# Neighbourhood attention in a two-layer backbone: scores as products over 128 stacked rows, or as products over 64 rows per head with both heads in turn

## The chip, the cores and the metric

The kernel runs on one core of a Trainium2 chip. Five engines of that core work in parallel: TensorE (PE in the profile; its weight loads are the rows PEld), VectorE (DVE), ScalarE (ACT), GpSimd (POOL) and SyncE (SP, which issues the DMAs). The metric is the device time of one execution in microseconds; lower is better.

## The reference, cut to what matters

Layer 0 is a differential attention and layer 1 a neighbourhood attention, both over 512 latent tokens and 256 context tokens with D = 1024; only layer 1 is touched by the change. It has 32 heads of 64 features:

```
q = rms_norm(q.reshape(bsz, n, NA_HEADS, NA_DH), qn_g)     # k likewise; v plain; z is the gate
k_band = kr[:, :, band_cols]                               # the keys near a block of queries
s = jnp.einsum('bnqhd,binxhd->bhnqix', q_r, k_band).astype(F32) * scale
s = jnp.where(valid[:, :, None, :], s + bias, -jnp.inf)
s_ctx = jnp.einsum('bnqhd,bkhd->bhnqk', q_r, k_c).astype(F32) * scale
p = jax.nn.softmax(jnp.concatenate([s, s_ctx], axis=-1), axis=-1)
out = einsum(p_band, v_band) + einsum(p_ctx, v_c)
out_l = (o_l * jax.nn.silu(z_l)) @ w_out
```

A block of 128 queries (16 columns of the grid by 8 rows) sees 256 latent keys (32 columns by 8 rows) and the 256 context keys. All is float32.

## The kernel before

**Numbers in two parts.** TensorE is used in the type fp32r. Each float32 operand is kept as a rounded part hi and a rest lo, and a product a·b is taken as hi·hi + hi·lo + lo·hi.

**Groups.** Layer 1 works in 16 groups of two heads (128 features). For each group `b_project` makes queries, keys, values and gate from the modulated tokens u (tiles `uhi`, `ulo`) and the group's weights (`whi`, `wlo`): 24 products a tile of 128 tokens, named `pj`. The weights come by DMA into `wraw`; ACT casts `whi` from it, and `wlo` = `wraw` - `whi` is made by DVE for half of them and by POOL for the other half. The tokens stand in three halves of 256: context (half 0), and two latent ones.

**Queries and keys.** DVE scales them by 1 / rms: `put_q` writes each head's 64 query features twice side by side (tile `qd`), `put_k` the keys once (tile `kk`). TensorE transposes them into the PSUM tiles `pq` and `pk`, so that features lie on partitions. `q_transposed` splits `pq` into `qT` [128, hi / lo, head, 256]: since a head's features were doubled, its 128 partitions hold the same 64 numbers twice. `k_transposed` splits `pk` into `KSb` [128, 2, 768], where a head's 128 partitions are hi on 64 and lo on the other 64. So a product over 128 partitions gives q·(k hi + k lo) at once.

**Scores.** `b_scores` runs once for each head (at half steps `s0` and `s1` of a group), with four blocks n of 128 queries each. A block's scores `Sb` fill one PSUM bank of 512 columns: 256 of the band and 256 of the context, each from two products (q hi, q lo), so 4 products of 256 columns a bank. Then DVE adds the bias (`bm`) and takes the row's least value (`nmb`), and ACT takes the exponentials into `pb` (n = 0 and 3) or `pp` (n = 1 and 2). `b_weights` transposes these on TensorE into `pwb`, ACT and DVE split them into `wTb`, and `b_values` multiplies with the values (`oTb`).

**What sets the order.** The program is first noted down as a list (class `Plan`; every instruction is issued from its line 277, so the profile shows L277 throughout). `Plan.order` then runs a list scheduler with estimated durations (`Op.estimate`), and every engine's instructions are issued in the order of that plan. On each engine this order is fixed; engines wait for each other by semaphores. PSUM has 8 banks: two for `pj`, three with tag `m` (`pq`, `pk`, `pwb`, `oTb` and others take turns), three for `Sb`. A new tile waits until the readers of the bank's earlier tile are done.

Of the kernel before, what the change touches and what calls it, by code (L numbers as in the profile page):

```python
# [18 lines left out]
P = 128  # L19
D = 1024  # L20
KT = 8
NG = 16
# [3 lines left out]
# token halves of 256: 0 = context, 1 and 2 = latent  # L26
# [10 lines left out]
# half steps of a projection between the parts of the attention  # L37
LAG = dict(pw=2.5, pv=1.5, po=0.5, py=1.5, qka=2, qkb=3, b1=2, b2=1.5, b3=1, bo=0.5, by=3)
# half steps at which the weights of the next groups are loaded, and the scores of a head begin
AT = dict(a0=8, a1=11, a2=11, a3=0, b0=6, b1=9, b2=9, b3=0, s0=5, s1=7, c0=2, c1=7, sa=0, cg=2, ch=9, c2=9, cv=1)  # L40
# [16 lines left out]
class Pool:  # L57
    """tiles of a pool by tag, with the number of buffers of each tag in one place"""
# [12 lines left out]
# ns from the end of an instruction to the start of one that needs it  # L71
# [12 lines left out]
class Op:  # L84
    """an instruction that waits for its place: its engine, what it touches, what it is likely to take"""
# [8 lines left out]
    def estimate(self, name):  # L94
        """ns"""
# [3 lines left out]
        if e == "PE":  # L99
            return 2.5 + n * (1 if reads[0].dtype == F32R else 2 if name == "transpose" else 4) / 2.4 if n > 2 else 260  # L100
# [15 lines left out]
class Rec:  # L116
    """an engine that notes its instructions"""
# [13 lines left out]
class Plan:  # L131
    """notes the program, then issues every engine's instructions in the order of a simulated run"""
# [48 lines left out]
    def order(self):  # L181
# [21 lines left out]
        def offer(i):  # L203
            """to its engine, unless a buffer is missing"""
# [19 lines left out]
        while len(out) < len(ops):  # L224
# [11 lines left out]
            # two of a tag at once, or a buffer gone since  # L236
# [4 lines left out]
            if e == "PE":  # L241
                # the tensor engine's clock is halved after an idle window
# [37 lines left out]
class K:  # L280
# [3 lines left out]
    # ------------------------------------------------------------ constants  # L284
# [19 lines left out]
    def load_vecs(self):  # L304
        """silu of both conditioning vectors, on every partition"""
# [23 lines left out]
    def mod_first(self):  # L329
        """scale and shift of layer 0 on the tensor engine; two steps per two tiles of features"""  # L330
# [7 lines left out]
        # columns: hi of both vectors, lo of both; their sums are the products with the weights' hi and lo  # L338
# [53 lines left out]
    def first_u(self, x, v, u, n, half):  # L392
        """two tiles of features of u hi / lo from x / rms"""
# [12 lines left out]
    def scaled(self, x, s, half):  # L406
        """x / rms, in place"""
# [4 lines left out]
    def mod_chunk(self, layer, ch):  # L412
        """e[:, ch] = (W^T chunk) . silu(c) for both vectors"""
# [9 lines left out]
    def mod_finish(self, layer, v, part):  # L423
        """part 0: shift b, 1: a = g (1 + scale), 2: gate"""
# [20 lines left out]
        # a token to a partition for the power, then to every partition  # L445
# [14 lines left out]
    def make_u(self, x, s, a, b):  # L460
        """x, 1 / rms -> u hi / lo"""
# [36 lines left out]
    def loads(self, Wn, W, layer, g, hs, on_pool):  # L498
        """weights of the next groups: the last part of g + 1 and the others of g + 2"""
# [5 lines left out]
    def project(self, o, W, u, j, kts, c=slice(0, 512)):  # L505
        """one tile of 128 tokens (tile j of a half) x the columns of a group"""
# [10 lines left out]
    # ------------------------------------------------------------ order of work: half steps  # L517
# [3 lines left out]
    def tick(self, step=0.5):  # L521
        """everything that is due by now"""
# [9 lines left out]
    def drained(self, gen, fill, hs):  # L532
        """what is left of the attention, with the steps of other work for the half steps that follow"""
# [7 lines left out]
    # ------------------------------------------------------------ per-head rms of q and k  # L541
# [5 lines left out]
    def rstd(self, sq):  # L547
        """squares [128, 2, 128] -> 1 / rms of each 64 columns, [128, 4]"""
# [8 lines left out]
    def put_q(self, t, rs, dst):  # L557
        """t [128, 128] (two heads) times rs, each head twice, into dst [128, 2, 2, 64]"""
# [9 lines left out]
    def q_transposed(self, qds):  # L568
        """two tiles [128, 2, 2, 64] -> [128, head, hi / lo, 256]"""
# [15 lines left out]
    def k_transposed(self, ks, KS, half):  # L585
        """two tiles [128, 128] -> stacks of hi and lo; head 0: (hi; lo), head 1: (lo; hi)"""
# [9 lines left out]

    def gate_z(self, pz, dst, mul=None):
# [5 lines left out]
    def gained(self, out, x, g):  # L603
        """[128, 2, 128] times a gain [128, 2, 64] of both heads"""
# [3 lines left out]
    def rope(self, ps, t):  # L608
        """(q | k) of a latent tile, rotated and times the norm's gains"""
# [14 lines left out]
    # ------------------------------------------------------------ layer 0: differential attention  # L624
    def a_tables(self):
# [35 lines left out]
    def a_tile(self, G, half, j, ps):  # L661
        """queries, keys, values and gate of a tile of 128 tokens"""
# [37 lines left out]
    def a_scores(self, g, G, half, j):  # L700
        """scores of 128 queries with both heads' keys, softmax and difference of the two"""
# [20 lines left out]
        # l0 (p0 / l0 - lambda p1 / l1); the norm that follows takes l0 out again  # L722
# [67 lines left out]
    # ------------------------------------------------------------ layer 1: neighbourhood attention  # L790
    def b_tables(self):
# [3 lines left out]
        # the scores come out negated: q's gain carries the sign  # L795
# [6 lines left out]
        for i in range(2):  # L802
            t = sb.tile([P, 2, 704], F32, name=f"pp{i}", tag="x8")
            nc.gpsimd.memset(t[:, :, 0:64], 0.0)
            nc.gpsimd.memset(t[:, :, 320:384], 0.0)
            self.pp += [t[:, 0], t[:, 1]]

    def b_project(self, G, U, W):
# [3 lines left out]
        for half in range(3):  # L812
            V = sb.tile([P, 2, 4, 64], F32R, name="Vb", tag="V")
            G["v"][half] = V
            if half == 0:
                # keys and values alone: both tiles share a bank
# [9 lines left out]
                ks = []  # L826
                for j in range(2):
                    ks.append(sb.tile([P, P], F32, name="kk", tag="kk"))
                    self.put_k(t1[:, j], rs[:, 2 * j : 2 * j + 2], ks[j])
                self.b_v(ps[:, :, P:256], V)  # L830
                self.later(LAG['qkb'], self.qk_transposed, G, half, None, ks)
                continue
            qds, ks = [], []
            for j in range(2):
# [14 lines left out]
                qd = sb.tile([P, 2, 2, 64], F32, name="qd", tag="qd")  # L849
                self.put_q(t1[:, 0:128], rs[:, 0:2], qd)  # L850
                qds.append(qd)
                self.gate_z(ps[:, 384:512], Z[:, j])
                k = sb.tile([P, P], F32, name="kk", tag="kk")
                self.put_k(t1[:, 128:256], rs[:, 2:4], k)
                ks.append(k)
                self.b_v(ps[:, 256:384].unsqueeze(1), V[:, j : j + 1])
                if j == 1:
                    self.later(LAG['qkb'], self.qk_transposed, G, half, qds, ks)
                yield

    def b_v_hi(self, ps, V):
        """values [.., 128] -> [.., 4, 64]: head 0: hi | lo, head 1: lo | hi"""
# [6 lines left out]
    def b_bias(self, g, h):  # L869
        """minus the bias, and what masks: one per place of a query block in the row; the last part is for the context"""  # L870
# [4 lines left out]
        for geo in range(3):  # L875
            o = 128 - 64 * geo
            nc.vector.tensor_tensor(bm[:, geo], self.mask[:, geo], raw[:, o : o + 256], ALU.subtract)
        nc.gpsimd.memset(bm[:, 3], 0.0)
        self.bm[h] = bm

    def b_scores(self, g, G, h):
        nc, sb = self.nc, self.sb
        KS, bm = G["KS"], self.bm[h]
        if h == 0:
            G["l"] = sb.tile([P, 4, 2], F32, name="lb", tag="lb")
            G["pair"] = sb.tile([P, 512], F32, name="pair", tag="oT")
        l = G["l"]
        pn = []
        for n in range(4):
            geo = (0, 1, 1, 2)[n]  # L890
            k0 = 256 + (0, 64, 192, 256)[n]
            S = self.psS.tile([P, 512], F32, name="Sb", tag="S")
# [5 lines left out]
            S2 = S.rearrange("p (a b) -> p a b", a=2)  # L898
            nm = sb.tile([P, 1], F32, name="nmb", tag="nm")
# [443 lines left out]
```

## Time and profile before

| | |
|---|---|
| median of 3 runs | 1830.32 us (1828.95 to 1832.27) |
| profiled execution, first to last instruction | 1827.4 us |
| median of the runs less that span | 2.9 us |
| TensorE busy | 1775.6 us, 97% |
| VectorE busy | 1487.5 us, 81% |
| ScalarE busy | 969.8 us, 53% |
| GpSimd busy | 602.2 us, 33% |
| groups of layer 1 | from about 1070 to 1745 us |

The profiled execution's own time is its span; what a run's time holds beyond the span (launch and end) is the 2.9 us. Busy is the union of an engine's instructions. A matmul's row shows from its start to its modelled end, which overlaps the next one's start, so the pace of TensorE is read from the distance of starts, not from the durations.

### The profile page before, as it was taken

What the parts mean: (1) busy time and instruction counts of PE and PEld (TensorE: products, weight loads), DVE (VectorE), ACT (ScalarE), POOL (GpSimd) and SP (SyncE); (2) the same over time, 40 slices, a digit from 0 to 9 for tenths busy, and PEclk for the clock granted to TensorE, in tenths of its full rate; (3) what the DMA queues carried; (4) which work ended last, traced back from release to release, by engine and by line L of the source; (5) the groups of instructions that cost most, each with busy time, mean ns of one, the idle gap of its engine ahead of it and who ended that gap; (6) DMA issues with size and microseconds to landing.
All of it is one profiled execution on the core that took longest, in us unless ns stands there. A gap on an engine that the chain in (4) does not pass through costs nothing.

```text
span 1827.4 us, 29430 instructions
## 1 busy us (share of the span) xinstructions
PE 1775.6 (97%) x10032; PEld 1509.2 (83%) x10032; DVE 1487.5 (81%) x3437; ACT 969.8 (53%) x2654; POOL 602.2 (33%) x915
## 2 busy tenths in 40 slices
PE   7899999999999999999999999999999999999999
PEld 3688888888888888888889988888888888888887
DVE  5888999898999999989858777777777777777863
ACT  4456555555555555556636455555555555555641
POOL 4544434444444444343100123333333333332100
PEclk9899999999999999999999999999999999999999
DMA  7401222121222222223556321111122211111423
GB/s 282 136 15 56 76 79 67 56 71 59 65 78 87 79 79 76 78 72 105 187 156 215 100 78 62 61 61 61 63 70 68 67 61 61 61 61 61 146 95 104
DMA packets 60774, 160.74 MB, mean 88 GB/s; under 512 B 7376, under 2 KB 22096, under 8 KB 59728
## 3 DMA queue, kind: packets, MB, share of 16 engines
q1 hardware_dynamic: 60624, 158.86, 26.7%
q8 instruction: 79, 1.29, 0.3%
q14 instruction: 71, 0.58, 0.1%
HBM read 144.68 MB, written 14.16 MB: 87 GB/s over the span
## 4 chain that ended last, share of the span: by engine, by line
PE 75%; DVE 15%; ACT 5%; issue 2%; POOL 2%; DMA 0%; SPq 0%; DVEq 0%; ACTq 0%; POOLq 0%
PE pj L277 40%; PE pjo L277 12%; PE oT L277 4%; PE S L277 4%; PE Sb L277 3%; PE pwb L277 3%; ACT pexp L277 3%; DVE wlo L277 3%; POOL ms L277 2%; PE pq L277 2%; DVE nm L277 2%; PE pw L277 1%; PE oTb L277 1%; DVE kk L277 1%; DVE t L277 1%
## 5 line engine op out<-in xcount | busy, mean ns | idle before, releaser
L277 PE MATMUL pj<-whi,ufirst 128*128 128x512 f32 x1536 | 524.6, 402 | 2.4 <-ACT ufirst L277 1.9
L277 PEld LDWEIGHTS pj<-whi,ufirst 128*128 128x128 f32 x1536 | 289.9, 189 | 58.1 <-ACT ufirst L277 2.5
L277 PE MATMUL pj<-wlo,ufirst 128*128 128x512 f32 x768 | 303.2, 395 | 0.0
L277 PE MATMUL pj<-wlo,uhi 128*128 128x512 f32 (+1 forms) x768 | 278.5, 363 | 12.1 <-DVE wlo L277 12.1
L277 PE MATMUL pj<-whi,uhi 128*128 128x512 f32 (+1 forms) x768 | 279.5, 364 | 0.0
L277 PE MATMUL pj<-whi,ulo 128*128 128x512 f32 (+1 forms) x768 | 276.3, 360 | 0.0
L277 ACT CAST whi<-wraw 128x512 fp32r<-128x512 f32 x352 | 209.3, 631 | 105.1 <-PE pjo L277 31.5
L277 DVE TENSOR_TENSOR wlo<-wraw,whi 128x512 fp32r<-128x512 f32 x288 | 220.6, 789 | 40.4 <-ACT whi L277 39.5
L277 POOL TENSOR_SCALAR ssk<-ssk 128x4 f32<-128x4 f32 x176 | 35.3, 201 | 556.9 <-DVE ssk L277 555.0
L277 ACT ACTIVATE pexp<-S,nm 128x768 f32<-128x768 f32 (+1 forms) x192 | 144.2, 758 | 127.8 <-DVE nm L277 127.7
L277 PE MATMUL pjo<-yhl,whi 128*128 128x512 f32 (+1 forms) x768 | 208.0, 357 | 0.0
L277 POOL TENSOR_TENSOR rsk<-ssk,mhalf 128x4 f32<-128x4 f32 x176 | 179.7, 1021 | 14.5
L277 PEld LDWEIGHTS pj<-wlo,uhi 128*128 128x128 f32 x768 | 145.2, 189 | 35.6 <-DVE wlo L277 19.0
L277 PEld LDWEIGHTS pj<-wlo,ufirst 128*128 128x128 f32 x768 | 145.8, 190 | 26.5
L277 PEld LDWEIGHTS pj<-whi,ulo 128*128 128x128 f32 x768 | 145.2, 189 | 17.9
L277 PEld LDWEIGHTS pj<-whi,uhi 128*128 128x128 f32 x768 | 145.3, 189 | 15.9
L277 PEld LDWEIGHTS pjo<-yhl,whi 128*128 128x128 f32 x768 | 134.8, 189 | 18.3
L277 DVE TENSOR_TENSOR wTb<-pwb,wTb 128x512 fp32r<-128x512 f32 (+2 forms) x192 | 101.1, 554 | 48.6 <-ACT wTb L277 47.7
L277 DVE TENSOR_REDUCE nm<-S 128x2 f32<-128x1536 f32 (+1 forms) x96 | 134.0, 1396 | 6.1 <-PE S L277 6.0
L277 PE MATMUL pjo<-yhl,wlo 128*128 128x512 f32 (+1 forms) x384 | 136.7, 356 | 0.0
L277 ACT CAST wTb<-pwb 128x512 fp32r<-128x512 f32 (+2 forms) x192 | 88.1, 487 | 88.8 <-PE pwb L277 87.2
L277 PE MATMUL S<-KS,qT 128*128 128x256 f32 (+1 forms) x640 | 132.8, 335 | 0.0
(161 smaller groups left out, 3552.5 us busy)
## 6 DMA issues: line engine op xcount, KB each, us to landing
wraw<-wa SPq DMA_DIRECT2D x64, 512.0 KB, 3.5
wraw<-wb SPq DMA_DIRECT2D x64, 512.0 KB, 3.9
modw<-modw SPq DMA_DIRECT2D x48, 512.0 KB, 3.8
wraw<-wo SPq DMA_DIRECT2D x24, 512.0 KB, 3.5
wraw<-wo SPq DMA_DIRECT2D x48, 256.0 KB, 3.2
yraw<-yd SPq DMA_DIRECT2D x14, 512.0 KB, 3.9
braw<-rpb SPq DMA_DIRECT2D x32, 192.0 KB, 2.4
yd<-yT SPq DMA_DIRECT2D x30, 128.0 KB, 1.9
```

What stands on the lines that cost most here:

```text
L277: op.f(*op.args, **op.kw)
```

## The change

Queries are kept once, like the keys. After scaling (`scaled_heads`, one instruction for q and k together) both are transposed into one PSUM tile `pqk`, and split into `qTn` [128, hi / lo, 256] and `KSb` [128, hi / lo, 768], in which head 0 lies on partitions 0 to 63 and head 1 on 64 to 127. A head's scores become three products over its 64 partitions (hi·hi, hi·lo, lo·hi), each with 512 keys (context and band) as one operand. `b_scores` is called once for both heads, notes their products in turn, and the estimate of such a product is halved.

```diff
@@ Op.estimate
         if e == "PE":
-            return 2.5 + n * (1 if reads[0].dtype == F32R else 2 if name == "transpose" else 4) / 2.4 if n > 2 else 260
+            half = 0.5 if reads[0].dtype == F32R and reads[0].shape[0] == 64 else 1
+            return 2.5 + half * n * (1 if reads[0].dtype == F32R else 2 if name == "transpose" else 4) / 2.4 if n > 2 else 260
@@ new
+    def scaled_heads(self, t, rs, dst):
+        self.nc.vector.tensor_tensor(dst.rearrange("p s (h d) -> p (s h) d", d=64), t.rearrange("p (s d) -> p s d", d=64),
+                                     rs.unsqueeze(2).broadcast_to([P, 4, 64]), ALU.mult)
+    def transposed(self, G, half, qks):
+        nc = self.nc
+        n = len(qks)
+        pt = self.pm.tile([P, n, 256], F32, name="pqk", tag="m")
+        for s in range(n):
+            for j in range(2):
+                nc.tensor.transpose(pt[:, s, j * P : j * P + P], qks[j][:, s] if n == 2 else qks[0][:, j], self.ident)
+        out = [(G["KS"][:, :, half * 256 : half * 256 + 256], pt[:, n - 1])]
+        if n == 2:
+            G["q"][half] = self.sb.tile([P, 2, 256], F32R, name="qTn", tag="qT")
+            out.append((G["q"][half], pt[:, 0]))
+        for o, x in out:
+            nc.scalar.copy(o[:, 0], x)
+        for o, x in out:
+            nc.vector.tensor_tensor(o[:, 1], x, o[:, 0], ALU.subtract)
@@ b_project, latent halves (the context half likewise, keys alone)
-                qd = sb.tile([P, 2, 2, 64], F32, name="qd", tag="qd")
-                self.put_q(t1[:, 0:128], rs[:, 0:2], qd)
+                qk = sb.tile([P, 2, P], F32, name="qk", tag="qd")
+                self.scaled_heads(t1, rs, qk)
-                k = sb.tile([P, P], F32, name="kk", tag="kk")
-                self.put_k(t1[:, 128:256], rs[:, 2:4], k)
-                    self.later(LAG['qkb'], self.qk_transposed, G, half, qds, ks)
+                    self.later(LAG['qkb'], self.transposed, G, half, qks)
@@ b_scores, for each n
-            for c, k in ((0, k0), (256, 0)):
-                for i in range(2):
-                    nc.tensor.matmul(S[:, c : c + 256], qT[:, i, h, (n % 2) * P : (n % 2) * P + P],
-                                     KS[:, h, k : k + 256], start=(i == 0), stop=(i == 1))
+            for i, (x, y) in enumerate(((0, 0), (0, 1), (1, 0))):
+                for h in range(2):
+                    r = slice(64 * h, 64 * h + 64)
+                    k = KS[r, y, 0:512].rearrange("p (a b) -> p a b", a=2)
+                    k = type(k)(k.tensor, k.offset, (k.ap[0], (k0, 2), (1, 256)))
+                    nc.tensor.matmul(S[h], qT[r, x, (n % 2) * P : (n % 2) * P + P], k, start=(i == 0), stop=(i == 2))
@@ b_third
-        tmp = self.sb.tile([P, 512], F32, name="otmp", tag="pb")
+        tmp = self.sb.tile([P, 512], F32, name="otmp", tag="y")
@@ run
-                        if hs in (AT["s0"], AT["s1"]):
-                            self.b_scores(g, G, int(hs == AT["s1"]))
+                        if hs == AT["s0"]:
+                            self.b_scores(g, G)
```

The later steps of head 1 keep their distance by a new lag (`b1h=2`); the exponentials of n = 0 go into `pp` too; the order of band and context within a bank is swapped.

The plan puts TensorE's scores elsewhere. Before, in a group in the middle of layer 1, after the transposes of the next group's context keys, the first head's scores stand on TensorE so; the second head's follow in the same form some 30 rows later:

```order
L277 MATMUL pk<-ident,kk 128x128 x2
L277 MATMUL Sb<-KSb,qT 128x256 x12
L277 MATMUL pj<-whi,uhi 128x512
L277 MATMUL pj<-wlo,uhi 128x512
L277 MATMUL pj<-whi,ulo 128x512
L277 MATMUL pj<-whi,uhi 128x512
L277 MATMUL pj<-wlo,uhi 128x512
L277 MATMUL Sb<-KSb,qT 128x256 x4
```

Now the first block of both heads stands at that place so (a group at the start of layer 1, with tile numbers: 3368 is head 0's and 3369 head 1's tile of the first block, 3372 head 0's of the second):

```order
L279 MATMUL Sb_3368<-KSb_3228,qTn_3297 128x512
L279 MATMUL Sb_3369<-KSb_3228,qTn_3297 128x512
L279 MATMUL Sb_3368<-KSb_3228,qTn_3297 128x512
L279 MATMUL Sb_3369<-KSb_3228,qTn_3297 128x512
L279 MATMUL Sb_3368<-KSb_3228,qTn_3297 128x512
L279 MATMUL Sb_3369<-KSb_3228,qTn_3297 128x512
L279 MATMUL Sb_3372<-KSb_3228,qTn_3297 128x512 x3
```

The heads alternate in the first block; from the second block on, a head's three products stand together. Further on in the same group, the rest of the scores stand on TensorE so:

```order
L279 MATMUL Sb<-KSb,qTn 128x512 x3
L279 MATMUL pj<-wlo,uhi 128x512
L279 MATMUL pj<-whi,ulo 128x512
L279 MATMUL pj<-whi,uhi 128x512
L279 MATMUL Sb<-KSb,qTn 128x512 x3
L279 MATMUL pj<-wlo,uhi 128x512
L279 MATMUL Sb<-KSb,qTn 128x512 x3
L279 MATMUL pj<-whi,ulo 128x512
L279 MATMUL pj<-whi,uhi 128x512
L279 MATMUL Sb<-KSb,qTn 128x512 x3
```

What was two stretches of 16 products with one break in each is now six stretches a group, of 9, 3, 3, 3, 3 and 3, with products over 128 rows between them. Over the layer the plan has 98 such stretches with 384 products, of which 96 (six a group) alternate between the heads.

On DVE the order changes around the `wlo` of the next group's last two weight tiles, for which the next group's first projection waits. Before, at the end of a group's projections, DVE has:

```order
L277 TENSOR_TENSOR wTb<-pwb,wTb 128x256
L277 SCALAR_TENSOR_TENSOR Zb<-Zb,pj 128x128
L277 TENSOR_TENSOR qd<-t_3847,rsk 128x256
L277 TENSOR_TENSOR kk<-t_3847,rsk 128x128
L277 TENSOR_TENSOR Vb<-pj,Vb 128x128
L277 TENSOR_TENSOR wlo<-wraw,whi 128x512 x2
L277 TENSOR_TENSOR pair<-oTb,otmp 64x512
```

Now it has, in the same part of a group:

```order
L279 TENSOR_TENSOR KSb<-pqk,KSb 128x256
L279 TENSOR_TENSOR qTn<-pqk,qTn 128x256
L279 TENSOR_TENSOR wlo<-wraw,whi 128x512
L279 TENSOR_TENSOR qk<-t_3766,rsk 128x256
L279 TENSOR_TENSOR wTb<-pwb,wTb 128x384 x2
L279 TENSOR_TENSOR wTb<-pwb,wTb 128x256
L279 TENSOR_TENSOR wlo<-wraw,whi 128x512
L279 TENSOR_TENSOR wTb<-pwb,wTb 128x512
L279 TENSOR_TENSOR wlo<-wraw,whi 128x512
L279 TENSOR_REDUCE ssk<-sqk 128x4
```

Before, the two `wlo` stand behind the work on the last projected tile (`Zb`, `qd`, `kk`, `Vb`); now the last two `wlo` of this piece, which are the same two weight tiles, stand ahead of that tile's first instruction on DVE (`ssk`).

## Rows read from the trace of the kernel before

**Rows 1.** The page's first part: busy time, share of the span, instructions.

```profile
PE 1775.6 (97%) x10032; PEld 1509.2 (83%) x10032; DVE 1487.5 (81%) x3437; ACT 969.8 (53%) x2654; POOL 602.2 (33%) x915
```

**Rows 2.** Busy time by stretch: layer 1's groups; PE, PEld, DVE, ACT, POOL, PE clock, DMA.

```profile
1070.00:1720.00 650.00, 625.83 (x3757) 545.41 (x3757) 506.63 (x1182) 344.34 (x900) 196.56 (x258) 1.00 0.20 66
```

**Rows 3.** Waits of PE in that stretch: total us, times, longest us.

```profile
PE pj L277 <- DVE wlo L277: 12.1, 25, 0.6
PE pwb L277 <- DVE qT L277: 12.1, 14, 0.9
```

**Rows 4.** Timeline of PE in one group: start us, us, instructions merged.

```profile
1302.59 0.40 PE L277 MATMUL pj<-whi,uhi 128*128 128x512 f32 x1
...
1305.34 0.64 PE L277 MATMUL Sb<-KSb,qT 128*128 128x256 f32 x4
1305.82 0.60 PE L277 MATMUL pq<-ident,qd 128*128 128x128 f32 x4
1306.26 0.38 PE L277 MATMUL pk<-ident,kk 128*128 128x128 f32 x2
```

**Rows 5.** Timeline of PE at the two waits of the same group.

```profile
1309.25 1.30 PE L277 MATMUL oTb<-wTb,Vb 128*128 128x512 f32 x6
1311.41 0.30 PE L277 MATMUL pwb<-ident,pb 128*128 128x128 f32 x1 [0.86 <-DVE qT L277]
...
1320.65 0.27 PE L277 MATMUL pwb<-ident,pb 128*128 128x128 f32 x1
1321.31 0.39 PE L277 MATMUL pj<-wlo,uhi 128*128 128x256 f32 x1 [0.38 <-DVE wlo L277]
```

**Rows 6.** Timeline of PE in layer 0's start: products over 4 rows between others.

```profile
73.11 0.40 PE L277 MATMUL pj<-wlo,ufirst 128*128 128x512 f32 x1
73.44 0.60 PE L277 MATMUL pmod<-both,erow 4*128 4x2 f32 x4
73.97 0.73 PE L277 MATMUL pj<-whi,ufirst 128*128 128x512 f32 x2
74.54 0.40 PE L277 MATMUL pj<-wlo,ufirst 128*128 128x512 f32 x1
```

**Rows 7.** Timeline of PE's weight loads there.

```profile
73.44 0.52 PEld L277 LDWEIGHTS pmod<-both,erow 4*128 4x128 f32 x4 [0.37 <-issue]
```

**Rows 8.** Timeline of PE at 1032 us: products over 128 rows between others.

```profile
1032.82 0.40 PE L277 MATMUL pj<-whi,ulo 128*128 128x512 f32 x1
1033.06 0.61 PE L277 MATMUL ss<-ident,nr 128*128 128x128 f32 x4
1033.42 0.47 PE L277 MATMUL pj<-whi,uhi 128*128 128x512 f32 x1
...
1033.96 0.40 PE L277 MATMUL pj<-whi,ulo 128*128 128x512 f32 x1
```

**Rows 9.** Groups of PE over the span: count, busy us, mean ns, idle before.

```profile
L277 PE MATMUL Sb<-KSb,qT 128*128 128x256 f32 x512 | 74.1, 287 | 0.0
...
L277 PE MATMUL pq<-ident,qd 128*128 128x128 f32 x320 | 53.0, 275 | 1.1 <-DVE qT L277 0.3 <-DVE qd L277 0.3
...
L277 PE MATMUL pk<-ident,kk 128*128 128x128 f32 x192 | 37.6, 272 | 0.0
```

**Rows 10.** Groups of DVE and ACT in 1070 to 1720 us, same columns.

```profile
L277 DVE TENSOR_TENSOR wlo<-wraw,whi 128x512 fp32r<-128x512 f32 x61 | 66.1, 1106 | 16.5 <-ACT whi L277 16.0
...
L277 DVE CUSTOM_DVE_ANT_1 Sb<-Sb,bm 128x512 f32<-128x512 f32 x90 | 60.5, 714 | 4.9 <-PE Sb L277 4.4
...
L277 DVE TENSOR_TENSOR kk<-t,rsk 128x128 f32<-128x128 f32 x87 | 46.6, 549 | 8.5 <-PE pk L277 8.5
...
L277 ACT ACTIVATE pp<-Sb,nmb 128x512 f32<-128x512 f32 x60 | 40.7, 685 | 44.8 <-DVE nmb L277 44.8
...
L277 DVE TENSOR_TENSOR KSb<-pk,KSb 64x256 fp32r<-64x256 f32 x88 | 37.2, 422 | 2.2
...
L277 DVE TENSOR_TENSOR qT<-pq,qT 128x512 fp32r<-128x512 f32 x29 | 19.6, 677 | 0.0
```

More of the change, by code (lines that the diff above doesn't have):

```diff
@@ L35 @@
             oT=1, y=1, yT=1, sq=1, t2=1, braw=1, tab=1, tab2=1)
-LAG = dict(pw=2.5, pv=1.5, po=0.5, py=1.5, qka=2, qkb=3, b1=2, b2=1.5, b3=1, bo=0.5, by=3)
-AT = dict(a0=8, a1=11, a2=11, a3=0, b0=6, b1=9, b2=9, b3=0, s0=5, s1=7, c0=2, c1=7, sa=0, cg=2, ch=9, c2=9, cv=1)
+LAG = dict(pw=2.5, pv=1.5, po=0.5, py=1.5, qka=2, qkb=3, b1=2, b1h=2, b2=1.5, b3=1, bo=0.5, by=3)
+AT = dict(a0=8, a1=11, a2=11, a3=0, b0=6, b1=9, b2=9, b3=0, s0=5, c0=2, c1=7, sa=0, cg=2, ch=9, c2=9, cv=1)
 FILL_A, FILL_B = (0, 1, 2, 3, 5, 7, 9, 11, 13, 15, 16, 17), (2, 4, 6, 8, 10, 11, 12, 13)
@@ L802, in b_tables @@
         for i in range(2):
[L803 to L806, printed above, removed]
+            t = sb.tile([P, 1792], F32, name=f"pp{i}", tag="x8")
+            a, b = t[:, 0:640], t[:, 640:1280]
+            for m in (a, b):
+                nc.gpsimd.memset(m[:, 256:320], 0.0)
+                nc.gpsimd.memset(m[:, 576:640], 0.0)
+            self.pp.append((t[:, 1280:1792], a, b))
     def b_project(self, G, U, W):
@@ L825, in b_project @@
                 self.gained(t1, ps[:, :, 0:P], self.gb[:, 1:2].broadcast_to([P, 2, 64]))
[L826 to L829, printed above, removed]
+                k = sb.tile([P, 2, P], F32, name="qk", tag="qd")
+                self.scaled_heads(t1.rearrange("p s d -> p (s d)"), rs, k)
                 self.b_v(ps[:, :, P:256], V)
-                self.later(LAG['qkb'], self.qk_transposed, G, half, None, ks)
+                self.later(LAG['qkb'], self.transposed, G, half, [k])
                 continue
-            qds, ks = [], []
+            qks = []
             for j in range(2):
@@ L876, in b_bias, with b_scores @@
             o = 128 - 64 * geo
-            nc.vector.tensor_tensor(bm[:, geo], self.mask[:, geo], raw[:, o : o + 256], ALU.subtract)
-        nc.gpsimd.memset(bm[:, 3], 0.0)
+            nc.vector.tensor_tensor(bm[:, geo + 1], self.mask[:, geo], raw[:, o : o + 256], ALU.subtract)
+        nc.gpsimd.memset(bm[:, 0], 0.0)
         self.bm[h] = bm
-    def b_scores(self, g, G, h):
+    def b_scores(self, g, G):
         nc, sb = self.nc, self.sb
[L883 to L888, printed above, removed]
+        KS = G["KS"]
+        l = sb.tile([P, 4, 2], F32, name="lb", tag="lb")
+        G.update(l=l, pair=sb.tile([P, 512], F32, name="pair", tag="oT"))
+        pn = [], []
         for n in range(4):
@@ L891, in b_scores @@
             k0 = 256 + (0, 64, 192, 256)[n]
-            S = self.psS.tile([P, 512], F32, name="Sb", tag="S")
+            S = [self.psS.tile([P, 512], F32, name="Sb", tag="S") for _ in range(2)]
             qT = G["q"][1 + n // 2]
-            for c, k in ((0, k0), (256, 0)):
-                for i in range(2):
-                    nc.tensor.matmul(S[:, c : c + 256], qT[:, i, h, (n % 2) * P : (n % 2) * P + P],
-                                     KS[:, h, k : k + 256], start=(i == 0), stop=(i == 1))
@@ L898, in b_scores @@
-            S2 = S.rearrange("p (a b) -> p a b", a=2)
-            nm = sb.tile([P, 1], F32, name="nmb", tag="nm")
-            nc.vector.tensor_tensor_reduce(out=S2, in0=S2, in1=bm[:, geo : 4 : 3 - geo], op0=ALU.add, op1=ALU.min,
-                                           scale=1.0, scalar=BIG, accum_out=nm)
-            if n in (1, 2):
-                p = self.pp[2 * h + n - 1]
-                dst = p[:, 64:704].rearrange("p (a b) -> p a b", b=320)[:, :, 0:256]
-            else:
-                p = sb.tile([P, 512], F32, name="pb", tag="pb")
-                dst = p.rearrange("p (a b) -> p a b", a=2)
@@ L908, in b_scores @@
-            nc.scalar.activation(dst, S2, AF.Exp, bias=nm, scale=-1.0, accum_out=l[:, n, h : h + 1])
-            pn.append(p)
-        if g + 1 < NG:
-            self.b_bias(g + 1, h)
-        self.later(LAG['b1'], self.b_first, g, G, h, pn)
+            for i, (x, y) in enumerate(((0, 0), (0, 1), (1, 0))):
[4 more added lines that the diff above has]
+                    nc.tensor.matmul(S[h], qT[r, x, (n % 2) * P : (n % 2) * P + P], k, start=(i == 0), stop=(i == 2))
@@ new lines, in b_scores @@
+            for h in range(2):
+                S2 = S[h].rearrange("p (a b) -> p a b", a=2)
+                nm = sb.tile([P, 1], F32, name="nmb", tag="nm")
+                nc.vector.tensor_tensor_reduce(out=S2, in0=S2, in1=self.bm[h][:, 0 : geo + 2 : geo + 1], op0=ALU.add, op1=ALU.min,
+                                               scale=1.0, scalar=BIG, accum_out=nm)
+                p = self.pp[h][n] if n < 3 else sb.tile([P, 512], F32, name="pb", tag="pb")
+                if n in (1, 2):
+                    dst = p.rearrange("p (a b) -> p a b", b=320)[:, :, 0:256]
+                else:
+                    dst = p.rearrange("p (a b) -> p a b", a=2)
+                nc.scalar.activation(dst, S2, AF.Exp, bias=nm, scale=-1.0, accum_out=l[:, n, h : h + 1])
+                pn[h].append(p)
@@ L914, in b_weights @@
+        for h in range(2):
+            if g + 1 < NG:
+                self.b_bias(g + 1, h)
+            self.later(LAG['b1'] + h * LAG['b1h'], self.b_first, g, G, h, pn[h])
     def b_weights(self, pn, kts):
@@ L921, in b_weights @@
             for n in ns:
-                if kt >= 4:
-                    o = (384 if n in (1, 2) else 256) + (kt - 4) * P
-                else:
-                    o = (kt - (0, 0, 1, 2)[n]) * P
+                o = (kt - 4) * P if kt >= 4 else 256 + (kt - (0, 0, 1, 2)[n]) * P
                 nc.tensor.transpose(pw[:, n * P : n * P + P], pn[n][:, o : o + P], self.ident)
```

3 lines of the change are left out of this document (1 added, 2 removed).

## The prediction

> **What bounds the kernel now.** I read the busy shares first, then the stretch that the change touches, then TensorE's waits in it, then its pace. Over the span TensorE is busy 97%, DVE 81% [rows 1]. Layer 1's groups run from about 1070 to 1745 us, 42 us each. In the 650 us of them that the windows view cuts out, TensorE is busy 625.8 us, DVE 506.6 us (78%) and ACT 344.3 us, at a granted clock of 1.00, the level of 2.4 GHz [rows 2]. TensorE's idle 24.2 us are all accounted for by two waits: 12.1 us in 25 waits for `wlo`, and 12.1 us in 14 waits, one a group, of a transpose into `pwb` for DVE's `qT` [rows 3]. So here a change is worth what it does to TensorE's own time and to these two waits; DVE and ACT have room.
>
> TensorE's pace is read from the distance of starts. Twelve `pj` products of 512 columns stand between 1302.59 and 1305.34 us: 0.229 us each. Four `Sb` products of 256 columns take 1305.34 to 1305.82: 0.120 each. Four transposes take 1305.82 to 1306.26: 0.11 each [rows 4].
>
> **The scores' products.** Before, 512 of 256 columns [rows 9] at 0.120 us: 61.4 us. Now 384 of 512 columns over 64 rows. The trace has no product over 64 rows. Bounds from the nearest rows: a product costs at least half of 0.229 us, if its neighbour on the other 64 rows streams beside it, and at most 0.229 us, if each goes alone; for less than a half nothing speaks, since only two groups of 64 rows exist. Which holds is decided by the order. Only 96 products alternate between the heads; I take the half for them (0.115 us, about the 0.11 us at which transposes follow each other; 11.0 us), with 22.0 us as the other end. The other 288 stand in threes of one head, on the same 64 rows, with nothing on the other rows beside them; they must cost 0.229 us, 66.0 us. Together 77.0 us, **+15.6 us**. Had all alternated it would be 44.2 us and a gain of 17.2.
>
> **The change between 64 and 128 rows.** The trace shows what it costs to go from products over all 128 rows to products over few rows and back. At 73.11 us there are a `pj`, four `pmod` products over 4 rows, and two `pj`, until 74.54: 1.43 us [rows 6]. At 1032.82 the same number of `pj` around four small products over all 128 rows takes until 1033.96: 1.14 us [rows 8]. The difference is 0.29 us a round trip. It is no wait for data: the weight load of the first `pmod` starts 0.33 us after the `pj` instead of beside it, and the row calls the 0.37 us before it "issue", a wait for nothing that the profile shows [rows 7]. Of the 0.33 us, 0.229 is the `pj`'s own pace and 0.10 is extra, as if the array first ran empty. Since the load then begins only after the stream, its 0.11 us lie bare as well; on the way back the two `pj` from 73.97 to 74.54 take 0.57 us instead of 0.46, the same 0.11. Small products are paced by their loads anyway, so they hide one of the bare loads; around a stretch of 512-column products each side should cost 0.10 + 0.11, a round trip 0.41 us.
>
> The Trainium skill says the same in its page "TensorEngine Tiling (Array Packing)", section "Key Properties": changing the tiling mode drains TensorE, while another tile of the same mode doesn't. The trace agrees with the first half, by these 0.29 us; no run so far shows the second. The page gives no price; by the row the drain is worth +28 to +40 us in all, which is what makes the change slow.
>
> The order has 98 stretches of 64-row products, each with a change in and a change out. At 0.41 us: **+40.3 us**; at the directly read 0.29 us: 28 us; were it free, 0. I take 0.41, since almost all of these stretches stand between `pj` products of 512 columns and consist of such.
>
> **Transposes.** `pq` 320 and `pk` 192 [rows 9]. A group had 8 + 6 in layer 1 and has 10 `pqk` now, so 64 fewer in 16 groups, at 0.11 us: **-7.0 us**. They run at the full pace between other work of TensorE, so all of it counts.
>
> **DVE and ACT.** In each group 2 `qT` of 677 ns, 6 `KSb` of 422, 6 `kk` of 549 [rows 10] and 4 `qd` go, and 5 scalings and 5 subtractions of 256 columns come; taking a `KSb` row's 422 ns for each of these ten (256 columns too) and for the four `qd`, DVE loses 1.35 + 2.53 + 3.29 + 1.69 - 4.22 = 4.6 us of its 33 a group. I cost this at nothing by itself: TensorE, not DVE, ends the stretches. Its worth is in the two waits.
>
> **The wait for `qT`.** The transpose into `pwb` needs a third bank of tag `m`, and `pq`, `pk` and `oTb` hold all three until DVE has split `pq`. From 1309.25 six `oTb` products need 4 x 0.229 + 2 x 0.120 us, until 1310.41; the transpose comes at 1311.41 [rows 5]. So a wait costs 1.0 us, somewhat more than the 0.86 that is shown as idle, since the modelled end of a product hides some. Now queries and keys share one bank, and their last reader is a 256-column subtraction in place of `qT`, `KSb` and `KSb`. I take the wait as gone: **-14 us**. If DVE is late there after all, it is the next `pwb` that is late, and 0 is gained.
>
> **The wait for `wlo`.** The row at 1320.65 is a transpose of 0.11 us; the next product comes at 1321.31, so 0.55 us are lost where 0.38 are shown [rows 5]; 25 such waits, each 0.17 us above what is shown, make 12.1 + 4.3 = 16.4 us. The new order has these two `wlo` ahead of the last tile's work on DVE, which speaks for their coming in time. But a `wlo` takes 1106 ns here [rows 10], so a change of its place by one or two instructions doesn't secure it. I take half: **-8 us**, with 0 and -16 as the ends.
>
> **The three score banks.** A bank comes free after DVE (714 ns) and ACT (685 ns) [rows 10], one after the other, so a new bank is to be had each 0.9 us or so with what these read out. TensorE now needs one per three products and a change of rows, 0.69 + 0.41 us, plus the `pj` between. I cost this at nothing; what covers it is TensorE's own slower pace; without that cover each of the five later banks of a group could cost some tenths of a us.
>
> **The sum.** 15.6 + 40.3 - 7.0 - 14 - 8 = +26.9 us on the span of 1827.4 us, so 1854.3 us. The median of the runs lies 2.9 us above that span; with it the prediction is **1857 us**, 1.5% slower.
>
> **Rivals.**
> - *Free change of rows.* The 0.29 us are read from products over 4 rows of another type; that fp32r products over 64 rows behave otherwise is possible. Then the sum is 15.6 - 7.0 - 14 - 8 = -13.4 us, 1817 us, and between 1809 (both waits gone) and 1839 us (both stay). This is the other side; it decides from 0.14 us a round trip (13.4 / 98) downwards. Rows 6 to 8 speak against it.
> - *No overlap of the alternating products.* 11 us more: 1868 us. For it speaks only that nothing in the trace shows two products at once.
> - *Bare weight loads.* The Trainium skill, "TensorE: Matmul & The Clock Gate", Part 3, says that a weight load runs beside a product in flight only where their row groups differ. As a mechanism here: in a stretch of three products of one head, two loads would wait for the product ahead. With the 0.11 us of a load, 2 x 96 x 0.11 = 21 us more, 1878 us. Against it: the `pj` products, all on the same rows, follow each other in 0.229 us, which leaves no 0.11 us bare [rows 4].
> - *The scores' own stretch isn't on the path.* If TensorE's longer scores only used up idle time, nothing would change, 1830 us. Against it: of 42 us a group, TensorE idles 1.6, and not there.
>
> **How the numbers follow.** Likeliest is the sum above, with the change of rows between 0.29 and 0.41 us and the `wlo` wait between its ends: 1837 to 1865 us, and up to 1876 if new waits take the place of the two old ones; chance 0.62. No overlap or bare loads on top: 0.13, 1868 to 1890 us. Free change of rows: 0.20, of which 0.15 end faster and 0.05 near no change. The last rival or a mix of small terms near no change: 0.05, of it 0.02 the same and 0.03 slightly slower. A difference of 0.2% (3.7 us) is about what a measurement of this kernel can tell from none. Faster 0.15, same 0.07, slower 0.78. The range takes in the likeliest case, the upper rivals but for their end, and the part of the free case nearest to it: 1824 to 1884 us.
>
> **What would show it.** After: at each of the 98 stretches the first `Sb` weight load stands some 0.3 us behind the last `pj`, with "issue" ahead of it, and so does the first `pj` load behind the last `Sb`. In the first block of a group six `Sb` starts lie within about 0.7 us (right) or 1.4 us (no overlap); later threes lie 0.229 us apart, or 0.34 with bare loads. PE's wait for `qT` has no successor, that for `wlo` is smaller. Layer 0 and the last output projection take as long as before. The prediction is wrong if loads of either kind run beside products across the change of rows, or if a new wait of TensorE above 10 us appears in layer 1.

## The result, and the profile after

The changed kernel takes **1847.2 us** (median of 4 runs, 1845.86 to 1848.28), the kernel before 1829.64 us beside it: a ratio of 1.0094, with a 95% interval of 1.0082 to 1.0107. It is slower by 17.6 us, where the prediction said 27. The profiled span is 1844.1 us against 1827.4, 16.7 us more.

The page's first part, answering to [rows 1]; TensorE is busier, DVE and ACT less:

```profile
PE 1814.2 (98%) x9840; PEld 1491.9 (81%) x9840; DVE 1416.3 (77%) x3309; ACT 953.3 (52%) x2606; POOL 593.7 (32%) x919
```

Busy time by stretch, first most of layer 0, then the 650 us of layer 1's groups as in [rows 2] (PE, PEld, DVE, ACT, POOL, granted clock, DMA):

```profile
82.00:1050.00 968.00, 963.75 (x5365) 820.16 (x5364) 853.43 (x2003) 542.23 (x1591) 347.32 (x612) 1.00 0.28 89
...
1070.00:1720.00 650.00, 650.00 (x3520) 521.01 (x3517) 429.54 (x1043) 324.48 (x842) 191.82 (x255) 1.00 0.20 62
```

Layer 0 is as it was (963.57 us of PE in the same stretch before; the first scores of layer 1 begin at 1069.4 us, before at 1069.6). In the groups TensorE is now busy all the time: the view of its waits has no row left there, so both waits of [rows 3] are gone. Yet from the first scores of group 0 to those of group 14 it is 632.8 us, where it was 624.8. The loss is in TensorE's own pace. Its timeline in one group shows where:

```profile
1249.86 0.38 PE L279 MATMUL pqk<-ident,qk 128*128 128x128 f32 x2
1250.17 1.66 PE L279 MATMUL Sb<-KSb,qTn 64*128 64x512 f32 x9
1251.76 0.50 PE L279 MATMUL pj<-whi,uhi 128*128 128x512 f32 x1
1252.10 0.40 PE L279 MATMUL pj<-wlo,uhi 128*128 128x512 f32 x1
...
1253.25 0.39 PE L279 MATMUL pj<-whi,uhi 128*128 128x512 f32 x1
1253.57 0.96 PE L279 MATMUL Sb<-KSb,qTn 64*128 64x512 f32 x3
1254.46 0.50 PE L279 MATMUL pj<-wlo,uhi 128*128 128x512 f32 x1
1254.79 0.39 PE L279 MATMUL pj<-whi,ulo 128*128 128x512 f32 x1
```

From 1253.25 to 1254.79 us are five products of 512 columns, a `pj`, three `Sb` and a `pj`: 1.54 us, where five at 0.229 us would be 1.145. So this stretch costs **0.40 us** extra: 0.09 between the `pj` and the first `Sb` (0.32 apart), 0.20 in the three `Sb` up to the next `pj` (0.89 for 0.69), and 0.10 in that `pj` (0.33). The median of the 75 stretches of this kind is 1.55 us, 0.41 extra. No row calls it a wait: PE counts as busy throughout, because the products' modelled ends cover it. The weight loads' timeline shows it, as in [rows 7]:

```profile
1250.17 1.23 PEld L279 LDWEIGHTS Sb<-KSb,qTn 64*128 64x128 f32 x9 [0.17 <-issue]
1251.76 0.19 PEld L279 LDWEIGHTS pj<-whi,uhi 128*128 128x128 f32 x1 [0.36 <-issue]
1251.87 0.19 PEld L279 LDWEIGHTS pj<-wlo,uhi 128*128 128x128 f32 x1
...
1253.57 0.53 PEld L279 LDWEIGHTS Sb<-KSb,qTn 64*128 64x128 f32 x3 [0.35 <-issue]
1254.45 0.19 PEld L279 LDWEIGHTS pj<-wlo,uhi 128*128 128x128 f32 x1 [0.36 <-issue]
```

At each change between `pj` and `Sb` the loads stand some 0.35 us idle with "issue" ahead of them (0.17 behind the transposes, ahead of the nine), and the first load starts no earlier than its product; between two `pj` it starts a product's length ahead (the one at 1251.87 is for the product at 1252.10).

The first stretch has nine `Sb` and takes 1.59 us up to the next `pj`, less than nine times 0.229 (2.06). The single records say why: a product of head 0 and one of head 1 start 3 ns apart (1 to 4 ns in all 48 pairs of the run), and so in pairs at 1250.174, .509 and .744; then three of the second block follow alone at .977, 1251.213 and .437. Two products on different 64 rows do run at once, and one alone costs a full 0.23 us.

DVE's waits in these groups, longest in total first (columns as in [rows 3]), and three of its groups that answer to [rows 10]:

```profile
DVE Sb L279 <- PE Sb L279: 72.8, 75, 1.6
DVE ssk L279 <- ACT sqk L279: 55.2, 41, 2.7
DVE wTb L279 <- ACT wTb L279: 38.6, 71, 2.3
```

```profile
L279 DVE CUSTOM_DVE_ANT_1 Sb<-Sb,bm 128x512 f32<-128x512 f32 x90 | 63.4, 704 | 61.9 <-PE Sb L279 50.3 <-ACT pp L279 11.6
L279 DVE TENSOR_TENSOR wlo<-wraw,whi 128x512 fp32r<-128x512 f32 x55 | 46.4, 843 | 12.4 <-ACT whi L279 11.3
...
L279 DVE TENSOR_TENSOR KSb<-pqk,KSb 128x256 fp32r<-128x256 f32 x43 | 18.0, 418 | 1.8 <-ACT KSb L279 0.7
```

DVE now waits for TensorE's scores (for the one form of the row alone 50.3 us, before 4.4), not TensorE for DVE: the three score banks hold nothing up. A `wlo` fell from 1106 to 843 ns, which had not been forecast; experiment 4 shows that the new order alone brings such a fall.

From the first scores of group 14 to the end it was 133.0 us and is 141.9, +8.9 us in two groups and the last output projection, as much as the +8.0 in the 14 groups ahead. Those last groups had no wait to lose, so the cost stands there without the gain. They have a new one: the view of the waits from 1700 us on has no row before, and after it has this one, in the last output projection:

```profile
PE pjo L279 <- ACT whi L279: 1.8, 2, 1.5
```

### The profile page after: what moved, and what is told of

Its sections match the earlier page's. It is cut to its first block, busy times and chain, and to the rows that moved or that the text cites. A ratio compares the mean times of both kernels' runs of the same rounds, so it can differ in the third digit from the quotient of the medians.

```text
span 1844.1 us, 28936 instructions
## 1 busy us (share of the span) xinstructions
PE 1814.2 (98%) x9840; PEld 1491.9 (81%) x9840; DVE 1416.3 (77%) x3309; ACT 953.3 (52%) x2606; POOL 593.7 (32%) x919
## 4 chain that ended last, share of the span: by engine, by line
PE 83%; DVE 8%; ACT 4%; POOL 2%; issue 1%; DMA 1%; SPq 0%; DVEq 0%; ACTq 0%
PE pj L279 44%; PE pjo L279 12%; PE Sb L279 5%; PE S L279 4%; PE oT L279 4%; PE oTb L279 4%; PE pwb L279 3%; ACT pexp L279 2%; POOL ms L279 2%; PE pw L279 2%; PE pq L279 1%; DVE nm L279 1%; PE pqk L279 1%; DVE y L279 1%; DVE mjunk L279 1%
## 5 line engine op out<-in xcount | busy, mean ns | idle before, releaser
L279 DVE TENSOR_TENSOR wlo<-wraw,whi 128x512 fp32r<-128x512 f32 x288 | 205.0, 730 | 37.3 <-ACT whi L279 35.8
L279 ACT ACTIVATE sqk<-pj 128x256 f32<-128x256 f32 x176 | 67.4, 383 | 186.6 <-PE pj L279 181.5
```

Source lines behind the costliest of these rows:

```text
L279: op.f(*op.args, **op.kw)
```

## The experiments

The theory (A) was the prediction's: each stretch of 64-row products costs about 0.4 us for the two changes of rows, and the waits' end pays for part of it. The main rival (B) was that the time comes from the products and the scores' new order themselves, not from the change of rows. All times are medians beside the kernel before on the same chip (1830.75 us for the first four, 1830.18 for the other three).

### 1. The same order, products over 128 rows

```diff
-            half = 0.5 if reads[0].dtype == F32R and reads[0].shape[0] == 64 else 1
+            half = 0.5 if out.tensor.name.startswith("Sb") else 1
...
-                    r = slice(64 * h, 64 * h + 64)
+                    r = slice(0, P)
```

Each score here sums over both heads' features. Everything else, the plan's order included, is the changed kernel's.

> Every instruction and its order as in the changed kernel; only the scores' products run over all 128 partitions, so that no product over 64 rows is left (each head's scores then sum over both heads' features, so the output is another). Theory A (each of the 98 stretches of 64-row products costs about 0.40 us for the change of rows in and out): 98 x 0.40 = 39 us less, and 96 products that no longer run in pairs cost 11 us more, so 1847 - 28 = 1819 us, with the weight loads of the scores beside the product ahead of them. Theory B (the change of rows costs nothing that counts; the added time is that of 64-row products that run alone): no gain, the lost pairs cost 11 us, 1858 us.

Measured: **1816.17 us**, ratio to before 0.9924 (0.9912 to 0.9936); 31.0 us below the changed kernel, as A has it. TensorE's timeline at the two places shown above:

```profile
1242.80 2.31 PE L279 MATMUL Sb<-KSb,qTn 128*128 128x512 f32 x9
1244.95 0.39 PE L279 MATMUL pj<-whi,uhi 128*128 128x512 f32 x1
...
1246.31 0.39 PE L279 MATMUL pj<-whi,uhi 128*128 128x512 f32 x1
1246.54 0.84 PE L279 MATMUL Sb<-KSb,qTn 128*128 128x512 f32 x3
1247.22 0.39 PE L279 MATMUL pj<-wlo,uhi 128*128 128x512 f32 x1
1247.44 0.39 PE L279 MATMUL pj<-whi,ulo 128*128 128x512 f32 x1
```

The same five products take 1.13 us from 1246.31 to 1247.44, not 1.54: the 0.40 us are gone, and with them the pairs (nine now take 2.15 us). The first `Sb` load now starts with the `pj` ahead of its product, and no "issue" stands before it:

```profile
1246.31 0.64 PEld L279 LDWEIGHTS Sb<-KSb,qTn 128*128 128x128 f32 x3
```

The 31.0 us and the 11.0 us that the pairs had saved make 42 us over 98 stretches, **0.43 us** each. This settles the direction: with the rows unchanged the same edit is faster than before.

### 2. The heads' products not in turn

```diff
-            for i, (x, y) in enumerate(((0, 0), (0, 1), (1, 0))):
-                for h in range(2):
+            for h in range(2):
+                for i, (x, y) in enumerate(((0, 0), (0, 1), (1, 0))):
```

> The changed kernel with the three products of head 0 noted ahead of those of head 1, so that no two of different heads alternate; the number of stretches of 64-row products stays about the same. If two alternating products over different 64 rows run beside each other at 0.115 us each, the 96 that alternated now cost 0.229 us: 11 us more, 1858 us. If they did not overlap, no change, 1847 us.

Measured: **1849.01 us**, ratio 1.0102 (1.0087 to 1.0118), an interval that overlaps the changed kernel's. The number is that of "no overlap", but the rows refute it:

```profile
1250.03 1.66 PE L279 MATMUL Sb<-KSb,qTn 64*128 64x512 f32 x9
1251.62 0.50 PE L279 MATMUL pj<-whi,uhi 128*128 128x512 f32 x1
```

Nine products still take 1.59 us. In the program head 0's three stand first, then head 1's; in the single records each of head 1's stands 10 ns behind one of head 0's (1250.032 and .042, .367 and .377, .602 and .612), and only the last pair has the semaphore updates that a head's third product makes. Both of the expected outcomes fall: the products overlap without being issued in turn, here with three of one head ahead of three of the other in one stretch.

### 3. All four blocks in pairs

Each block's six products wait in the plan until head 0's exponential of the block before, so that a block goes in one stretch:

```diff
+            nc.fence = {freed} if n else set()
             for i, (x, y) in enumerate(((0, 0), (0, 1), (1, 0))):
...
+            nc.fence = set()
...
+                if h == 0:
+                    freed = len(nc.ops) - 1
```

> The changed kernel with the six products of a block of queries held back in the plan until both heads' banks are free, so that all 384 alternate, in 4 stretches a group in place of 6. Theory A: the products fall from 77 to 384 x 0.115 = 44 us, and about 34 round trips of 0.40 us go, 14 us: 1847 - 47 = 1800 us. Theory B (no cost of the change of rows): only the 33 us, 1814 us. If TensorE has to wait for the score banks in between, less than either.

Measured: **1806.63 us** (1805.03 to 1810.74), ratio 0.9874 (0.986 to 0.9887). PE's timeline at one stretch, its waits in 1070 to 1720 us, and that stretch's windows row:

```profile
1246.20 0.39 PE L279 MATMUL pj<-wlo,uhi 128*128 128x512 f32 x1
1246.52 0.96 PE L279 MATMUL Sb<-KSb,qTn 64*128 64x512 f32 x6
1247.41 0.50 PE L279 MATMUL pj<-whi,ulo 128*128 128x512 f32 x1
1247.74 0.40 PE L279 MATMUL pj<-whi,uhi 128*128 128x512 f32 x1
```

```profile
PE pwb L279 <- DVE qTn L279: 2.7, 9, 0.4
PE pwb L279 <- DVE wTb L279: 1.3, 5, 0.3
PE pj L279 <- DVE wlo L279: 0.8, 1, 0.8
```

```profile
1070.00:1720.00 650.00, 645.21 (x3707) 524.05 (x3707) 446.95 (x1103) 340.85 (x886) 198.07 (x261) 1.00 0.20 70
```

Six products now take the 1.54 us (with two `pj`) that three took. There are 64 stretches instead of 98 and 384 paired products instead of 96, so A's saving is 34 x 0.40 + 144 x 0.229 = 47 us, and B's, without the first term, 33; 40.6 came. By itself this lies between the two. But TensorE has new waits, 4.8 us of idle time shown; by the distance of starts those between the first scores of group 0 and of group 14 lose about 8 us, and with them A's sum is 39.

### 4. Before, with both heads' scores at one place

```diff
-        self.later(LAG['b1'], self.b_first, g, G, h, pn)
+        self.later(LAG['b1'] + 2 * h, self.b_first, g, G, h, pn)
...
-                        if hs in (AT["s0"], AT["s1"]):
-                            self.b_scores(g, G, int(hs == AT["s1"]))
+                        if hs == AT["s0"]:
+                            for h in range(2):
+                                self.b_scores(g, G, h)
```

> The kernel before with one thing of the change: head 1's scores are noted right behind head 0's at the same half step, with head 1's later steps two half steps later, as in the changed kernel. Queries, keys and products as before. If the two waits of TensorE (24 us shown, some 30 us of lost time) went because of the new order, they go here too: 1830 - 30 = 1800 us. If they went because DVE has 4.6 us less work a group and queries and keys share a bank, they stay: 1825 to 1832 us.

Measured: **1806.95 us**, ratio 0.9871 (0.9857 to 0.9884). Windows row, and PE's waits:

```profile
1070.00:1720.00 650.00, 645.57 (x3894) 566.06 (x3893) 488.72 (x1228) 356.93 (x932) 204.19 (x262) 1.00 0.21 71
```

```profile
PE pwb L277 <- DVE wTb L277: 2.0, 10, 0.3
PE pwb L277 <- DVE pair L277: 1.3, 7, 0.2
```

The waits for `qT` and `wlo` are gone, though queries are still kept twice, and still split by `qT`, `KSb`, `KSb`, and DVE has the same 3437 instructions: the order of the scores removes them. This alone is worth 24 us, more than half of what the changes of rows cost. The two new waits lose about 10 us by the distance of starts, more than the 3.3 shown, so the 30 us that were expected are not reached.

DVE's instructions are the same, but some are shorter, as these rows show beside [rows 10] (1106 and 549 ns before):

```profile
L277 DVE TENSOR_TENSOR wlo<-wraw,whi 128x512 fp32r<-128x512 f32 x65 | 51.4, 813 | 31.7 <-ACT whi L277 31.2
...
L277 DVE TENSOR_TENSOR kk<-t,rsk 128x128 f32<-128x128 f32 x88 | 31.4, 370 | 8.6 <-PE pk L277 8.6
```

So the faster `wlo` comes with the order of the scores; what makes it faster there was not tried.

### 5. Before, both heads at one place, 512 keys in one operand

Experiment 4 with the change's layout of a bank, over 128 rows, so two products of 512 columns a bank in place of four of 256 (the edits of the bias, the padding and the transposes that follow from the layout are left out here):

```diff
-            for c, k in ((0, k0), (256, 0)):
-                for i in range(2):
-                    nc.tensor.matmul(S[:, c : c + 256], qT[:, i, h, (n % 2) * P : (n % 2) * P + P],
-                                     KS[:, h, k : k + 256], start=(i == 0), stop=(i == 1))
+            k = KS[:, h, 0:512].rearrange("p (a b) -> p a b", a=2)
+            k = type(k)(k.tensor, k.offset, (k.ap[0], (k0, 2), (1, 256)))
+            for i in range(2):
+                nc.tensor.matmul(S, qT[:, i, h, (n % 2) * P : (n % 2) * P + P], k, start=(i == 0), stop=(i == 1))
```

> The kernel before with two things of the change: both heads' scores noted at one half step (1807 us alone), and 512 keys in one operand over 128 rows, so 256 products of 512 columns in place of 512 of 256 columns. Starts 0.229 us apart in place of 0.120: 58.6 us for 61.4, so 1807 - 3 = 1804 us. If the width of an operand doesn't matter, 1807 us.

Measured: **1805.46 us**, ratio 0.9862 (0.9848 to 0.9877). By the pace 256 x 0.229 in place of 512 x 0.120 us should save 2.8 us; 1.5 us were seen, and the interval overlaps that of experiment 4. It stays open whether this part has any worth.

### 6. Queries and keys in a bank each

```diff
-        pt = self.pm.tile([P, n, 256], F32, name="pqk", tag="m")
+        pt = [self.pm.tile([P, 256], F32, name="pqk", tag="m") for _ in range(n)]
...
```

> The changed kernel with the transposes of queries and of keys in a PSUM bank each, as before the change. If the wait for DVE went because queries and keys share a bank, about 14 us of it come back: 1861 us. If it went because of where the scores stand, no change: 1847 us.

Measured: **1846.83 us**, ratio 1.0092 (1.0076 to 1.0109), and PE has no wait in the groups. The wait for `qT` stays gone without the shared bank.

### 7. Two stretches a group

Experiment 3 with a fourth bank for scores, borrowed from tag `m` for head 1 of the odd blocks, and a fence before the third block only:

```diff
-            S = [self.psS.tile([P, 512], F32, name="Sb", tag="S") for _ in range(2)]
+            S = [self.pm.tile([P, 512], F32, name="Sb", tag="m") if n % 2 and h else self.psS.tile([P, 512], F32, name="Sb", tag="S") for h in range(2)]
...
+            nc.fence = {freed} if n >= 2 else set()
...
+                if n == 1:
+                    freed = len(nc.ops) - 1
```

> As the run with all products in pairs, but two blocks of queries make one stretch: a fourth score bank is borrowed from the three of tag m, and a group has 2 stretches of 12 products in place of 4 of 6. The products' time is the same. If a change of rows in and out costs 0.40 us, 32 fewer of them make 13 us: 1806.6 - 13 = 1794 us. If the price of a stretch lies in what stands in it and not in its ends, 1806 us. A wait of TensorE for the borrowed bank would take back part of the gain.

Measured: **1787.38 us**, ratio 0.9769 (0.9754 to 0.9783): 2.3% faster than before, the fastest here. One stretch, and the windows row:

```profile
1234.76 1.66 PE L279 MATMUL Sb<-KSb,qTn 64*128 64x512 f32 x12
1236.35 0.50 PE L279 MATMUL pj<-whi,uhi 128*128 128x512 f32 x1
```

```profile
1070.00:1720.00 650.00, 650.00 (x3818) 548.82 (x3815) 453.39 (x1129) 347.07 (x906) 195.78 (x260) 1.00 0.22 73
```

Twelve products in the 1.59 us that nine took, and no wait. It is 19.2 us under experiment 3, where 13 were expected; there are 29 stretches fewer, not 32 (35 in the whole trace, since the last group's first two blocks stand in four), and experiment 3's new waits, about 8 us, are gone too. The cost of a stretch is read better against the changed kernel, since neither has a wait here: from the first scores of group 0 to those of group 14 it is 580.2 us, 52.5 less than 632.8. Nine products a group that now run beside others make 14 x 9 x 0.229 = 28.9 us of it; the other 23.7 us over 56 stretches are **0.42 us** each, the third reading, beside 0.40 and 0.43.

## Why the prediction was right, and where it wasn't

The direction and the mechanism were right, and the time lies in the range; the sum was 10 us too high, chiefly by one term. The terms, with what the runs showed:

| step | forecast, us | shown, us |
|---|---|---|
| the scores' products | +15.6 | +15.6: pairs 1 to 4 ns apart, single ones 0.23 us, read directly |
| change of rows, 98 stretches | +40.3 (0.41 each; the product is 40.2) | +39 to +42 (0.40, 0.43, 0.42 each) |
| transposes | -7.0 | -7.0: 160 `pqk`, again 0.11 us apart |
| waits for `qT` and `wlo` | -14 and -8 | -14.7 and -18.7, by the distance of starts before |
| DVE, ACT, score banks | 0 | no wait of PE in the groups; +1.8 in the last output projection, for ACT |
| sum | +26.9 | +16 to +19, beside 16.7 measured |

**The change of rows** was sized from products of 4 rows in layer 0, and what was added to the 0.29 us read there, a bare load that was reasoned and not seen, was right: 0.41 forecast, 0.40 read. The sentence on where it is spent, half on each side, fits too: 0.09 ahead of the stretch, 0.10 behind it in the `pj`, and 0.20 between, where the two other halves lie. Experiment 1 shows it as a cause: taken away, the time falls by 31.0 us with nothing else in the order moved. So the rival "free change of rows" falls. Of the Trainium skill's page "TensorEngine Tiling (Array Packing)", section "Key Properties", the second half, that another tile of one mode doesn't drain the engine, had not been seen before; the trace agrees, as the pairs, which go from one head's rows to the other's, follow each other in the usual 0.23 us (1250.509 to .744), and so does the step from pairs to one head's products inside a stretch (.744 to .977).

**No overlap** falls by the pairs; that only alternation gives it, as the prediction assumed, falls by experiment 2. Since the plan parts the heads' later blocks, that error cost nothing here. **Bare weight loads** fall by the 0.23 us between single products on the same 64 rows. The `pj` loads too run beside a product on the same 128 rows (the one at 1251.87, beside the product of 1251.76). Here a rule and the rows differ: the Trainium skill, "TensorE: Matmul & The Clock Gate", Part 3, in its list of what overlaps, lets a load run beside a product only on other row groups (its text ahead of the list names the background weight buffer as well), and the measurement decides. **The scores not on the path** falls by experiment 1, where the scores' products alone move the time by 31 us.

**The mis-sized step** is "I take half: -8 us" for `wlo`. That wait went wholly, and it was larger than the upper end named there, 16.4 us. That end came from one wait with 0.38 us shown; the other kind, 13 of the 25, shows 0.61 in all but one case:

```profile
1321.91 0.48 PE L277 MATMUL pj<-whi,uhi 128*128 128x512 f32 x1
1322.99 0.38 PE L277 MATMUL pj<-wlo,uhi 128*128 128x256 f32 x1 [0.61 <-DVE wlo L277]
1323.22 0.28 PE L277 MATMUL pj<-whi,ulo 128*128 128x256 f32 x1
```

From 1321.91 to 1323.22 it is 1.31 us, where these two products take 0.43 without a wait (0.31, as a `pj` behind a transpose has it, and 0.12): 0.88 us lost. Read so, the 13 lose 11.1 us and the other 12 (0.64 each) 7.6, together 18.7. The 14 waits for `qT`, read the same way, lose 14.7. With the measured waits the sum is 15.6 + 40.3 - 7.0 - 14.7 - 18.7 + 1.8 = 17.3 us, beside 16.7 measured. The words on which half was taken, that a move "by one or two instructions doesn't secure it", looked at the move alone. In experiment 4, with the new order alone, the wait is gone too, in groups that are shorter than before (43.0 us from scores to scores, where it was 44.6) and with a `wlo` of 813 ns; how the faster `wlo` and its earlier place share in it was not separated.

**The step with a wrong reason** is the wait for `qT`. "Now queries and keys share one bank" was given as the cause, and -14 us as the size. Experiment 6 takes the shared bank away and the wait stays gone; experiment 4 leaves the queries' old layout and the wait goes too. So that this term came out at its size was luck: the order alone is enough to remove both waits, since the second head's scores no longer stand some 30 rows later. Which piece of that order frees which wait was not tried.

The prediction also calls a group 42 us long; from scores to scores it was 44.6. Nothing in its sum hangs on that.

The two ends of layer 1 show the two effects apart: +8.0 us over 14 groups, in which 84 stretches at 0.41 us, the products and the transposes make +42 and the waits take back 33.4 (all of them lie there); and +8.9 us behind them, where 14 stretches make 5.7 us, products and transposes 1.1 us, the new wait of `pjo` 1.8 us, and nothing is taken back. The prediction had the last output projection as long as before, and missed that wait.

The terms carry over to the best version: experiment 7 has all but a few of its 384 products in pairs (-17.2 us), 35 stretches (+14.4 at 0.41), the transposes (-7.0) and the waits (-33.4): -43.2 us on the span, measured 1784.3 - 1827.4 = -43.1. For experiment 3 they give -31.4, and with its new waits, about 8 us, -23.4, beside -24.1 between the medians; the span fell by only 18.4 in the profiled execution, which is 4 us above that kernel's median.

## What to carry to other kernels

Products over fewer rows are worth having only if the stretches in which they stand are counted: here each costs 0.40 to 0.43 us whether it holds three products or twelve, so twelve in one stretch win what three in each of four lose. Hold a stretch together by a bank more and an order that lets it run through, and put products of both row halves into it. And when an edit changes the order as well as the work, run the order alone: here it held 24 us of gain that the slower whole hid.

## What the runs showed of the hardware

- A TensorE that the profile shows busy for 650 of 650 us can still lose 0.40 us at each stretch of 64-row products among 128-row ones; only the distance of starts, or the gap in the weight loads marked "issue", shows it.
- The idle time shown for a wait of TensorE is less than what the wait costs: before, 39 waits show 24.2 us and lose 33.4 by the distance of starts.
- Products on different 64 rows start 1 to 4 ns apart when issued in turn, and 4 to 10 ns apart even where two others of the first head stand between them in the program (experiment 2). The Trainium skill's page "TensorE: Matmul & The Clock Gate", Part 3, has products start in program order; these records differ from it.
- Both heads' weight loads of a pair start 3 to 4 ns apart in the stretch at 1250.17 us, and cost no time of their own: in experiment 7 twelve products run at six products' pace.
- With the scores in another order and nothing else changed, DVE's `wlo` went from 1106 to 813 ns and its `kk` from 549 to 370 (experiment 4); the cause is open.
